# A third buffer for the weights, row adds moved to VectorE, and small products pinned late, in a hybrid attention and ConvFFN step

## The chip, the cores and the metric

The kernel runs on 1 core of one Trainium2 chip. The metric is the device time of one execution in microseconds, as the median of several runs. Its engines are TensorE (PE in the profile, its weight loads PEld), VectorE (DVE), ScalarE (ACT), GpSimd (POOL) and SyncE (SP), whose queue here issues the DMAs.

## The reference

One layer of a streaming encoder, all in float32, on 512 prompt tokens and 32 sample tokens with cached keys and values:

```
h = rmsnorm(x) * g1
qa, ka, va, qb, kb, vb, ga, gb = split(h @ w_in)        # 1024 -> 6656
oa = sliding window attention (16 heads, 4 kv heads, ALiBi, sink), q and k normed per head
ob = chunk band attention (16 heads, learned bias by distance), q and k normed per head
x = x + (sigmoid(ga) * oa + sigmoid(gb) * ob) @ w_out   # 1024 -> 1024
u = (rmsnorm(x) * g2) @ w_up                            # 1024 -> 2 * 2816
c = conv_b + conv_w0 * u[t-2] + conv_w1 * u[t-1] + conv_w2 * u[t]   # causal, per channel
x = x + (gelu(c[first half]) * c[second half]) @ w_down # 2816 -> 1024
```

For the sample tokens u[-2] and u[-1] come from a cached state (`cache_ffn_conv`). The new keys and values and the last rows of u are returned too.

## The kernel before

**Layout and arithmetic.** Activations lie transposed: 128 channels on the partitions, the T = 544 tokens along the row, in two halves of 272. To keep float32 precision each operand of a matmul is split into a rounded high part and the rest, a low part, and each product is made of three matmuls: high x high, high x low, low x high (`triple`, L220).

**Weights.** A weight tile is 128 x 1024 (8 blocks of 128 x 128, one output block of 128 channels for all of D = 1024). `prep` (L192) takes three tiles from the pool `wp`: `w_raw` (loaded by SyncE), `w_hi` (cast by GpSimd up to the end of w_out, by ScalarE from w_up on) and `w_lo` (a subtraction on VectorE). The pool has two buffers of each. `weights()` (L213) hands out the next tile and sees that the tiles up to two behind it are begun. What `prep_next` issues has a lower priority by 300 places than what stands around it. There are 50 tiles of w_in, 8 of w_out, 44 of w_up, 6 of w_down; `dense` (L232) uses one of them in 48 matmuls (2 halves, 8 blocks, 3 each). All loads that go through `load` (L166) with the same kind keep their written order in SyncE's queue.

**Order of the work.** Instructions are traced in an order that a small planner (`Stream`, L69) sets for TensorE: between dense products it steps through attention tasks when their estimated latencies are over. A scheduler then orders each engine's queue by readiness in a simulated time, and by priority; engines work their queues off in that order.

**Start.** x is loaded in 8 row blocks, interleaved with the first two weight tiles. Each row block k is split into xh and xl at once (`row_split`, ScalarE and VectorE), without its norm: the first FIRST = 3 tiles are multiplied by x times gain only (`dense_first`, L271), and their six halves stay in six PSUM banks until rstd is there. `RowNorm.row` (L337) squares each x block on ScalarE and adds it to a running sum on the engine given (L398: GpSimd for blocks up to 4, VectorE for the rest); `finish` splits the sum and multiplies it by a matrix of ones, and rstd is made on ScalarE and VectorE (L312, L360, L361). Up to the eighth tile VectorE multiplies each result by rstd as it leaves PSUM (L290); then x itself is rescaled (L254) and split again (L327).

**ConvFFN.** 44 tiles of w_up, each followed by the convolution on VectorE, ScalarE and a few GpSimd instructions on `carry`, six small products of the cached state with the convolution's weights (L925 to L929) that depend on inputs alone. Gate and value products are split and kept. Of the 22 products the first REST = 6 are used directly; 16 form 8 pairs, whose seven factors (`make_pair`, L960) serve a Strassen-like form of w_down. EARLY pairs are made as soon as their products are there, the others behind the last gate. A split half of a pair or product lives in a home: first the 19 slots of pool `gp`, then slots of `fp`, then the 16 tiles of xh and xl once w_up is through, then `fp` again. Pool `fp` has 50 slots of 128 x 544, in which x1 (8 slots) and working tiles lie as well.

**End.** First the 6 direct products (48 blocks of w_down), then the pairs: for each of four pairs of output rows (m), 4 units of 7 factors, each factor 6 matmuls. `sums` (L1007) loads a unit's weights, forms s13, s2 and s4 with three VectorE additions, and casts and subtracts each of the seven operands into a slot of `fp` (L1020, L1021), traced up to 10 operands ahead. Behind the last unit of each m the seven PSUM banks are combined into x1 and stored (`leave`, L1072).

Of the kernel before, what the change touches and what calls it, by code (L numbers as in the profile page):

```python
# [8 lines left out]
F32 = mybir.dt.float32  # L9
F32R = mybir.dt.float32r  # L10
AF = mybir.ActivationFunctionType
ALU = mybir.AluOpType
# [14 lines left out]
GT = FF // 128  # L27
PAIRS = 8
REST = GT - 2 * PAIRS
EARLY = 5  # L30
UNITS = PAIRS // 2
H = T // 2
EPS = 1e-6
# [110 lines left out]
def body(ctx, tc, a, o):  # L144
# [4 lines left out]
    V, G = nc.vector, nc.gpsimd  # L149
    rr = lambda t: t.bitcast(F32)  # L150

    const = ctx.enter_context(tc.tile_pool(name="const", bufs=1))
    wp = ctx.enter_context(tc.tile_pool(name="wp", bufs=2))
    xp = ctx.enter_context(tc.tile_pool(name="xp", bufs=1))
    psd = ctx.enter_context(tc.tile_pool(name="psd", bufs=3, space=PSUM))
    psa = ctx.enter_context(tc.tile_pool(name="psa", bufs=5, space=PSUM))
# [9 lines left out]
    def load(out, src, kind="x"):  # L166

        with tc.issue_after(loads[kind].ins) if kind in loads else nullcontext():
            loads[kind] = nc.sync.dma_start(out=out, in_=src)
# [13 lines left out]
    sources = [a["w_in"][m] for m in plan] + [a["w_out"][m] for m in range(8)]  # L183
# [6 lines left out]
    state = {"prepped": 0, "used": 0}  # L190

    def prep(n):  # L192
        raw = wp.tile([128, 1024], F32, name="w_raw", bufs=2)
        hi = wp.tile([128, 1024], F32R, name="w_hi")
        lo = wp.tile([128, 1024], F32R, name="w_lo")
        W[n] = (hi, lo)
        cuts = (0, 256, 1024) if n < 2 else (0, 1024)
        for c in map(slice, cuts, cuts[1:]):
            load(raw[:, c], sources[n][:, c])
            if n < ffn:  # L200
                G.tensor_scalar(hi[:, c], raw[:, c], 1.0, 1.0, ALU.mult, ALU.mult)  # L201
            else:
                nc.scalar.copy(hi[:, c], raw[:, c])  # L203
            V.tensor_tensor(lo[:, c], raw[:, c], rr(hi)[:, c], ALU.subtract)  # L204
            yield

    def prep_next():
        with tc.high_priority(LATER):
            for _ in prep(state["prepped"]):
                pass  # L210
        state["prepped"] += 1

    def weights():  # L213
        n = state["used"]
        state["used"] += 1
        while state["prepped"] < min(n + 3, len(sources)):
            prep_next()
        return W.pop(n)

# [12 lines left out]
    def dense(evac, pool=None):  # L232
        if not norm_done:
            return dense_first(evac)
        if early:
            pool = psa
            early.clear()
        w = weights()
        for s, (c0, cn) in enumerate(HALVES):
            ps = bank(pool or psd)  # L240
            for k in range(KC):
                triple(ps, w, k, c0, cn, k == 0, k == KC - 1)
                if k == KC - 1:
                    evac(s, c0, cn, ps[:, :cn])
                if xt:
                    rescale(state["used"], s, k)
                pe.step()
# [23 lines left out]
    def dense_first(evac):  # L271


        early.append((evac, weights()))
        if len(early) < (FIRST if xt else 2):
            return
        halves = [(bank(psd if i < 3 else psa), early[i // 2][1], i % 2) for i in range(2 * len(early))]
        interleaved(halves[:3], range(KC))
        for h in halves[3:]:
            interleaved([h], range(KC))  # L280
        while not norm_done:
            pe.idle()
        for i, (ps, _, s) in enumerate(halves):
            c0, cn = HALVES[s]
            early[i // 2][0](s, c0, cn, ps[:, :cn])
# [80 lines left out]
    att = ctx.enter_context(ExitStack())  # L366
# [9 lines left out]
    xt = [slot() for _ in range(KC)]  # L376
    load(n1, a["n1"])
    w = [prep(0), prep(1)]
    for step in START.split():
        n = int(step[1])  # L380
# [14 lines left out]
    norm = RowNorm(sp, ap)  # L395
    rstd = norm.r
    for k in range(KC):
        norm.row(xt[k], G if k <= 4 else V)  # L398


    def head_norm(gi, write):
# [468 lines left out]

    lag = 2
    w0, w1 = weights(), weights()
    halves = [(bank(psd), w0, 0), (bank(psd), w0, 1), (bank(psd), w1, 0), (bank(psa), w1, 1)]
    for k in range(KC):
# [8 lines left out]
    interleaved(halves[3:], range(KC))  # L883
    att.close()

    fp = att.enter_context(tc.tile_pool(name="fp", bufs=50, reuse_waits="tile"))
    ft = att.enter_context(tc.tile_pool(name="ft", bufs=1, reuse_waits="tile"))
    x1 = [fp.tile([128, T], F32, name="s") for _ in range(KC)]
    for m in range(KC):
# [1 line left out]
    norm = RowNorm(fp, ft)  # L891
# [29 lines left out]
    carry = ft.tile([128, UT, 2], F32, name="carry")  # L921
    per = lambda name: cols[:, slice(*COL[name])]
    state_c = per("cc").rearrange("p (m r) -> p m r", r=2)
    t = ft.tile([128, UT], F32, name="t_c")
    for r in range(2):  # L925
        G.tensor_tensor(carry[:, :, r], per("cw0"), state_c[:, :, r], ALU.mult)
        G.tensor_tensor(carry[:, :, r], carry[:, :, r], per("cb"), ALU.add)
    G.tensor_tensor(t, per("cw1"), state_c[:, :, 1], ALU.mult)
    G.tensor_tensor(carry[:, :, 0], carry[:, :, 0], t, ALU.add)  # L929

    def conv(m, n, done):
        u = us[n % 2]
# [20 lines left out]
    rest, pairs = [], []  # L953
    homes = [gp] * 19 + [fp] * (7 * EARLY + 2 * REST - 19) + [f"x{p}{k}" for k in range(KC) for p in "hl"]

# [4 lines left out]
    def make_pair(v1, v2):  # L960
        b11, b12, b21, b22 = (v[:, c:c + H] for v in (v1, v2) for c in (0, H))
        t13, t24 = (fp.tile([128, T], F32, name="s") for _ in range(2))
        first, *wide = home(), (home(), home()), (home(), home()), (home(), home())
        nc.scalar.copy(first[:, :H], b11)
        V.tensor_tensor(first[:, H:], b11, rr(first)[:, :H], ALU.subtract)
        split(*wide[0], v2)
        V.tensor_tensor(t13[:, :H], b11, b12, ALU.subtract)
        V.tensor_tensor(t13[:, H:], b12, b22, ALU.subtract)
        split(*wide[1], t13)
        V.tensor_tensor(t24[:, :H], b22, t13[:, :H], ALU.add)  # L970
        V.tensor_tensor(t24[:, H:], b21, t24[:, :H], ALU.subtract)
        split(*wide[2], t24)
        ops = {"b11": (first[:, :H], first[:, H:])}
        for names, hl in zip((("b21", "b22"), ("t1", "t3"), ("t2", "t4")), wide):
            for e, name in enumerate(names):
                ops[name] = tuple(x[:, e * H:e * H + H] for x in hl)
        pairs.append(ops)

    late = []
    for n, i in enumerate(gate_order):  # L980
# [6 lines left out]
        def gate(c, part=part, n=n):  # L987
# [7 lines left out]
            late.append(v)  # L995
            if n % 2 and len(pairs) < EARLY:
                make_pair(*late)
# [8 lines left out]

    def sums():  # L1007
        for n in range(KC // 2 * UNITS):
            raw = wp.tile([128, 1024], F32, name="w_raw", bufs=2)
            load(raw, a["w_pair"][n])  # L1010
            wc, wd, wa, wb = (raw[:, 256 * e:256 * e + 256] for e in range(4))
            s13, s24 = (fp.tile([128, 2, 256], F32, name="s") for _ in range(2))
            s1, s3, s2, s4 = s13[:, 0], s13[:, 1], s24[:, 0], s24[:, 1]
            V.tensor_tensor(s13, raw[:, 256:768].rearrange("p (e c) -> p e c", e=2),
                            wc.unsqueeze(1).to_broadcast([128, 2, 256]), ALU.add)
            V.tensor_tensor(s2, s1, wa, ALU.add)
            V.tensor_tensor(s4, s2, wb, ALU.add)
            for x in (wa, s2, s3, s1, wb, wd, s4):
                w = fp.tile([128, 2, 256], F32R, name="s")
                nc.scalar.copy(w[:, 0], x)  # L1020
                V.tensor_tensor(w[:, 1], x, rr(w)[:, 0], ALU.subtract)  # L1021
                ready.append(w)
                yield

    ready = []
    making = sums()

    def operand(n, ahead=10):
# [203 lines left out]
```

## Time and profile before

| | |
|---|---|
| median of 3 runs | 923.89 us (923.56 to 924.41) |
| profiled execution | 924.88 us, span 923.0 us |
| TensorE busy | 898.6 us (97%), 7085 matmuls |
| VectorE busy | 723.6 us (78%), 1471 instructions |
| ScalarE busy | 542.2 us (59%) |
| GpSimd busy | 379.1 us (41%), 578 instructions |
| chain that ended last, by engine | PE 76%, DVE 9%, ACT 4%, POOL 3%, issue 2% |

Times count from the start of the span. A busy share of TensorE counts overlapping matmuls, so it tells idle time and not speed. "Idle before" with an engine's name is the time that an engine stood still ahead of an instruction, and what released it.

### The profile page before, as it was taken

What the parts mean: (1) busy time and instruction counts of PE and PEld (TensorE: products, weight loads), DVE (VectorE), ACT (ScalarE), POOL (GpSimd) and SP (SyncE); (2) the same over time, 40 slices, a digit from 0 to 9 for tenths busy, and PEclk for the clock granted to TensorE, in tenths of its full rate; (3) what the DMA queues carried; (4) which work ended last, traced back from release to release, by engine and by line L of the source; (5) the groups of instructions that cost most, each with busy time, mean ns of one, the idle gap of its engine ahead of it and who ended that gap; (6) DMA issues with size and microseconds to landing.
All of it is one profiled execution on the core that took longest, in us unless ns stands there. A gap on an engine that the chain in (4) does not pass through costs nothing.

```text
span 923.0 us, 18908 instructions
## 1 busy us (share of the span) xinstructions
PE 898.6 (97%) x7085; PEld 884.4 (96%) x7085; DVE 723.6 (78%) x1471; ACT 542.2 (59%) x1285; POOL 379.1 (41%) x578
## 2 busy tenths in 40 slices
PE   8879999999999999999999999999999999999998
PEld 7879899989989999999999999999999999999998
DVE  7799876868888888998866558768777776886996
ACT  5568777778878777777764244344444443534542
POOL 6534457465876777766541103221222221100100
PEclk9999999999999999999999999999999999999999
DMA  6222222322334443434415222222222222332342
GB/s 216 83 82 88 71 90 85 101 81 75 109 118 122 135 124 109 129 110 136 133 59 168 89 92 92 92 77 85 92 93 92 84 87 83 96 101 81 119 145 67
DMA packets 40012, 94.38 MB, mean 102 GB/s; under 512 B 4944, under 2 KB 16240, under 8 KB 39920
## 3 DMA queue, kind: packets, MB, share of 16 engines
q1 hardware_dynamic: 39920, 93.17, 31.8%
q8 instruction: 56, 0.92, 0.4%
q14 instruction: 36, 0.29, 0.1%
HBM read 80.48 MB, written 7.10 MB: 95 GB/s over the span
## 4 chain that ended last, share of the span: by engine, by line
PE 76%; DVE 9%; ACT 4%; POOL 3%; issue 2%; DMA 0%; DVEq 0%; POOLq 0%
PE ps L85 73%; PE ps L89 3%; ACT p L485 2%; DVE q L446 1%; DVE zn L422 1%; DVE p L501 1%; DVE w_lo L204 1%; POOL p L493 1%; DVE s L254 1%; DVE t_b L319 1%; DVE k L431 1%; POOL t_sql L414 1%; POOL z L421 1%; DVE pt_l L512 0%; DMA k<-k 0%
## 5 line engine op out<-in xcount | busy, mean ns | idle before, releaser
L85 PE MATMUL ps<-xh,w_lo 128*128 128x272 f32 x1536 | 446.3, 292 | 5.1 <-DVE w_lo L204 5.1
L85 PE MATMUL ps<-xh,w_hi 128*128 128x272 f32 x1536 | 446.0, 292 | 2.7 <-ACT z L412 1.7
L85 PE MATMUL ps<-xl,w_hi 128*128 128x272 f32 x1536 | 446.3, 291 | 0.8 <-DVE xl L327 0.8
L85 PEld LDWEIGHTS ps<-xh,w_lo 128*128 128x128 f32 x1536 | 291.6, 190 | 6.5 <-DVE w_lo L204 6.0
L85 PEld LDWEIGHTS ps<-xh,w_hi 128*128 128x128 f32 x1536 | 291.5, 190 | 4.8 <-ACT z L412 1.9
L85 PEld LDWEIGHTS ps<-xl,w_hi 128*128 128x128 f32 x1536 | 292.0, 190 | 2.1 <-DVE xl L327 1.7
L204 DVE TENSOR_TENSOR w_lo<-w_raw,w_hi 128x1024 fp32r<-128x1024 f32 (+2 forms) x112 | 143.2, 1279 | 30.8 <-ACT w_hi L203 18.3
L201 POOL TENSOR_SCALAR w_hi<-w_raw 128x1024 fp32r<-128x1024 f32 (+2 forms) x62 | 66.6, 1075 | 90.2 <-PE ps L85 70.3
L493 POOL TENSOR_SCALAR p<-p,rc 128x256 f32<-128x256 f32 (+3 forms) x128 | 74.2, 596 | 41.4 <-DVE rc L491 38.0
L203 ACT CAST w_hi<-w_raw 128x1024 fp32r<-128x1024 f32 x50 | 52.6, 1051 | 64.9 <-issue 36.1
L85 PE MATMUL ps<-s,w_hi 128*128 128x272 f32 x448 | 84.0, 288 | 0.0
L485 ACT ACTIVATE p<-p,nm 128x256 f32<-128x256 f32 (+3 forms) x128 | 65.4, 514 | 27.8 <-DVE nm L482 27.7
L938 POOL TENSOR_SCALAR state_u<-u 128x2 f32<-128x2 f32 x44 | 17.1, 388 | 148.7 <-DVE u L935 148.7
L85 PE MATMUL ps<-s 128*128 128x272 f32 (+1 forms) x483 | 71.3, 293 | 1.7 <-DVE s L372 1.7
L85 PEld LDWEIGHTS ps<-s,w_hi 128*128 128x128 f32 x448 | 70.1, 188 | 0.0
L935 DVE TENSOR_TENSOR u<-ps,rstd 128x272 f32<-128x272 f32 x88 | 38.5, 441 | 39.6 <-PE ps L85 37.0
L85 PEld LDWEIGHTS ps<-s 128*128 128x128 f32 x483 | 65.1, 190 | 2.2 <-DVE s L372 1.7
L85 PE MATMUL ps<-s,w_lo 128*128 128x272 f32 x224 | 63.8, 288 | 0.0
L85 PE MATMUL ps<-k,q 128*128 128x256 f32 (+2 forms) x256 | 52.1, 308 | 3.5 <-DMA k<-k 1.8
L414 POOL TENSOR_TENSOR t_sql<-t_sq,t_sqh 128x272 fp32r<-128x272 f32 x52 | 52.7, 1014 | 3.7
L421 POOL TENSOR_TENSOR z<-z,t_y 128x272 f32<-128x272 f32 x52 | 42.7, 822 | 23.9 <-ACT t_y L316 21.7
L512 DVE TENSOR_TENSOR pt_l<-ps,pt_h 128x512 fp32r<-128x512 f32 (+1 forms) x80 | 45.6, 602 | 5.5 <-ACT pt_h L511 4.4
(166 smaller groups left out, 1635.1 us busy)
## 6 DMA issues: line engine op xcount, KB each, us to landing
w_raw<-in_w_in SPq DMA_DIRECT2D x50, 512.0 KB, 3.4
w_raw<-in_w_up SPq DMA_DIRECT2D x44, 512.0 KB, 3.3
w_raw<-in_w_pair SPq DMA_DIRECT2D x16, 512.0 KB, 3.4
k<-k SPq DMA_DIRECT2D x40, 128.0 KB, 2.3
bias<-in_rel SPq DMA_DIRECT2D x16, 256.0 KB, 2.7
w_raw<-in_w_out SPq DMA_DIRECT2D x8, 512.0 KB, 3.5
s<-in_x SPq DMA_DIRECT2D x15, 272.0 KB, 5.7
w_raw<-in_w_down SPq DMA_DIRECT2D x6, 512.0 KB, 3.3
```

Of the source, the lines that this page charges most:

```text
L85: return self.nc.tensor.matmul(out, lhsT=lhsT, rhs=rhs, **kw)
L89: return self.nc.tensor.transpose(out, src, ident)
L201: G.tensor_scalar(hi[:, c], raw[:, c], 1.0, 1.0, ALU.mult, ALU.mult)
L203: nc.scalar.copy(hi[:, c], raw[:, c])
L204: V.tensor_tensor(lo[:, c], raw[:, c], rr(hi)[:, c], ALU.subtract)
L414: G.tensor_tensor(sql, sq, rr(sqh), ALU.subtract)
L421: G.tensor_tensor(z, z, y, ALU.mult)
L485: act(p[:, sl], p[:, sl], AF.Exp, bias=nm[:, t:t + 1], accum_out=sm[:, t:t + 1])
L493: G.tensor_scalar(p[:, sl], p[:, sl], rc[:, t:t + 1], 1.0, ALU.mult, ALU.mult)
L512: V.tensor_tensor(l[:, :n], ps[:, :n], rr(h)[:, :n], ALU.subtract)
L935: V.tensor_tensor(u[:, 2 + c0:2 + c0 + cn], ps, rstd2[:, c0:c0 + cn], ALU.mult)
L938: G.tensor_scalar(state_u[:, m, 0:2], u[:, NP:NP + 2], 1.0, 1.0, ALU.mult, ALU.mult)
```

## The change

Three buffers instead of two for w_raw, w_hi and w_lo (12 KB more of each SBUF partition); each `weights()` begins tiles up to three behind the one handed out. The `fp` pool shrinks from 50 to 44 slots, EARLY from 5 to 4, and the sums of the pair weights move from two `fp` slots into a buffer of `w_lo`. All seven adds of the squares of x run on VectorE. The six small products on GpSimd are each pinned behind what was traced before on that engine.

```diff
-EARLY = 5
+EARLY = 4
...
-    wp = ctx.enter_context(tc.tile_pool(name="wp", bufs=2))
+    wp = ctx.enter_context(tc.tile_pool(name="wp", bufs=3))
...
-        raw = wp.tile([128, 1024], F32, name="w_raw", bufs=2)
+        raw = wp.tile([128, 1024], F32, name="w_raw")
...
-        while state["prepped"] < min(n + 3, len(sources)):
+        while state["prepped"] < min(n + 4, len(sources)):
...
-        norm.row(xt[k], G if k <= 4 else V)
+        norm.row(xt[k], V)
...
-    fp = att.enter_context(tc.tile_pool(name="fp", bufs=50, reuse_waits="tile"))
+    fp = att.enter_context(tc.tile_pool(name="fp", bufs=44, reuse_waits="tile"))
...
+    late_g = lambda *x: tc.keep_in_program_order(G.tensor_tensor(*x))
     for r in range(2):
-        G.tensor_tensor(carry[:, :, r], per("cw0"), state_c[:, :, r], ALU.mult)
-        G.tensor_tensor(carry[:, :, r], carry[:, :, r], per("cb"), ALU.add)
-    G.tensor_tensor(t, per("cw1"), state_c[:, :, 1], ALU.mult)
-    G.tensor_tensor(carry[:, :, 0], carry[:, :, 0], t, ALU.add)
+        late_g(carry[:, :, r], per("cw0"), state_c[:, :, r], ALU.mult)
+        late_g(carry[:, :, r], carry[:, :, r], per("cb"), ALU.add)
+    late_g(t, per("cw1"), state_c[:, :, 1], ALU.mult)
+    late_g(carry[:, :, 0], carry[:, :, 0], t, ALU.add)
...
-            raw = wp.tile([128, 1024], F32, name="w_raw", bufs=2)
+            raw = wp.tile([128, 1024], F32, name="w_raw")
...
-            s13, s24 = (fp.tile([128, 2, 256], F32, name="s") for _ in range(2))
+            both = wp.tile([128, 4, 256], F32, name="w_lo")
+            s13, s24 = both[:, 0:2], both[:, 2:4]
```

## Rows read from the trace of the kernel before

**Rows 1.** The page's first part: busy us, share, instructions.

```profile
PE 898.6 (97%) x7085; PEld 884.4 (96%) x7085; DVE 723.6 (78%) x1471; ACT 542.2 (59%) x1285; POOL 379.1 (41%) x578
```

**Rows 2.** Stretches: length, busy PE, PEld, DVE, ACT, POOL, granted clock, DMA, GB/s.

```profile
12.00:24.00 12.00, 10.18 (x71) 8.85 (x69) 11.43 (x12) 5.71 (x11) 11.69 (x12) 1.00 0.52 172
24.00:36.00 12.00, 9.85 (x61) 9.39 (x62) 8.82 (x15) 5.06 (x13) 5.19 (x7) 0.86 0.35 106
...
60.00:72.00 12.00, 9.07 (x63) 8.85 (x62) 11.73 (x30) 9.92 (x23) 1.04 (x1) 0.89 0.18 55
...
480.00:560.00 80.00, 80.00 (x638) 79.92 (x637) 49.97 (x77) 32.92 (x49) 12.79 (x19) 1.00 0.34 114
```

**Rows 3.** TensorE's timeline: start, us, instruction, idle before it and its releaser.

```profile
24.26 0.52 PE L85 MATMUL ps<-s,ones 128*128 128x272 f32 x2 [0.51 <-ACT s L351]
25.21 0.40 PE L85 MATMUL ps<-xh,w_hi 128*128 128x272 f32 x1 [0.43 <-POOL w_hi L201]
27.76 0.40 PE L85 MATMUL ps<-xh,w_lo 128*128 128x272 f32 x1 [1.46 <-DVE w_lo L204]
...
51.07 0.37 PE L85 MATMUL ps<-t_sqh,bdiag 128*128 128x272 f32 x1 [1.42 <-POOL w_hi L201]
...
69.08 0.44 PE L85 MATMUL ps<-xh,w_lo 128*128 128x272 f32 x1 [2.93 <-DVE w_lo L204]
```

**Rows 4.** Stretches of 2 us, columns as in rows 2.

```profile
28.00:30.00 2.00, 2.00 (x12) 2.00 (x12) 2.00 (x5) 0.35 (x2) 0.00 (x0) 0.58 0.58 182
...
32.00:34.00 2.00, 2.00 (x18) 2.00 (x17) 0.62 (x2) 1.91 (x5) 1.25 (x3) 1.00 0.35 131
...
70.00:72.00 2.00, 2.00 (x10) 2.00 (x10) 2.00 (x7) 1.83 (x5) 0.00 (x0) 0.50 0.85 264
```

**Rows 5.** GpSimd's timeline at the start, columns as in rows 3.

```profile
13.20 5.64 POOL L342 TENSOR_TENSOR s<-s 128x544 f32<-128x544 f32 x3
18.81 1.48 POOL L926 TENSOR_TENSOR carry<-cols 128x44 f32<-128x44 f32 x2
...
24.11 2.52 POOL L201 TENSOR_SCALAR w_hi<-w_raw 128x1024 fp32r<-128x1024 f32 x2
...
35.01 1.05 POOL L201 TENSOR_SCALAR w_hi<-w_raw 128x1024 fp32r<-128x1024 f32 x1 [1.68 <-PE ps L85]
```

**Rows 6.** Instructions on tile s, 0 to 40 us: duration ns min/median/max, starts, forms.

```profile
L327 DVE SCALAR_TENSOR_TENSOR xl<-s,n,xh x9: 501/795/1880, 4.3 to 20.1; 128x544 fp32r<-128x544 f32 x7, 128x272 fp32r<-128x272 f32 x2
...
L342 POOL TENSOR_TENSOR s<-s x4: 1356/1764/1960, 10.4 to 17.1; 128x544 f32<-128x544 f32 x4
...
L342 DVE TENSOR_TENSOR s<-s x3: 712/800/976, 20.8 to 22.7; 128x544 f32<-128x544 f32 x3
```

**Rows 7.** VectorE's timeline at the start, columns as in rows 3.

```profile
15.76 5.11 DVE L327 SCALAR_TENSOR_TENSOR xl<-s,n,xh 128x544 fp32r<-128x544 f32 x4
...
21.92 1.62 DVE L342 TENSOR_TENSOR s<-s 128x544 f32<-128x544 f32 x2
...
30.28 0.50 DVE L361 TENSOR_SCALAR rstd<-rstd 128x272 f32<-128x272 f32 x2
```

**Rows 8.** Timelines of TensorE, ScalarE and VectorE in the pair products.

```profile
835.40 11.06 PE L85 MATMUL ps<-s 128*128 128x272 f32 x87
...
836.36 0.41 ACT L1020 CAST s<-w_raw 128x256 fp32r<-128x256 f32 x1 [9.69 <-PE ps L85]
...
843.56 0.42 DVE L1021 TENSOR_TENSOR s<-s 128x256 fp32r<-128x256 f32 x1 [0.32 <-ACT s L1020]
...
846.16 0.68 DVE L1014 TENSOR_TENSOR s<-w_raw 128x512 f32<-128x512 f32 x1
```

**Rows 9.** VectorE's groups, 800 to 835 us: busy us, mean ns, idle before.

```profile
L204 DVE TENSOR_TENSOR w_lo<-w_raw,w_hi 128x1024 fp32r<-128x1024 f32 x5 | 6.1, 1223 | 1.1 <-ACT w_hi L203 1.1
...
L431 DVE TENSOR_TENSOR xl<-s,xh 128x544 fp32r<-128x544 f32 x3 | 2.2, 719 | 0.0
```

**Rows 10.** GpSimd's timeline as the convolutions begin.

```profile
551.03 0.19 POOL L938 TENSOR_SCALAR state_u<-u 128x2 f32<-128x2 f32 x1 [27.74 <-DVE u L935]
```

## The prediction

> **What bounds the kernel now.** I read the page's busy shares first, then the stretches, then TensorE's waits, then the queues of the engines it waits for. TensorE is busy 898.6 of 923.0 us, so the idle time there, 24.4 us, is nearly all that can be won [rows 1]. The stretches show where it lies: from 480 us on TensorE is never idle (80.00 of 80.00 us in the row shown), so nothing that the change does there can save time, it can only cost. In 12 to 24, 24 to 36 and 60 to 72 us it is idle for 1.82, 2.15 and 2.93 us [rows 2]. In the timeline each long gap of the first 84 us names a weight tile or the row sum: 0.51 us for the sum (L351), 0.43 and 1.46 us for the high and low part of the third tile, 1.42 us for a high part at 51 us, 2.93 us for a low part at 69 us [rows 3]. Two of these gaps cost more than themselves: behind them the granted clock falls to 0.58 and 0.50, which is about its lower level of 1.2 GHz, and TensorE starts 12 and 10 matmuls in 2 us where it starts 18 at 1.00 [rows 4].
>
> Why are the weights late? Two buffers: the third tile's high part goes where the first tile's was, so GpSimd can't cast it before TensorE has left the first tile. And GpSimd is then still behind: three of its row adds fill 13.20 to 18.84, the small products for the cached state follow at 18.81, and the cast starts at 24.11 [rows 5]. VectorE is slowed at the same time.
>
> **Part 1: the start, 8 to 36 us.** Third buffer: the third tile needs no release, so its load, cast and subtraction run while TensorE works on the first two. Removed on GpSimd in this stretch: 4 row adds (median 1.764 us each, [rows 6]) and six small products. Added on VectorE: 4 adds at 0.800 us (median, [rows 6]), 3.2 us. But a VectorE instruction with two operands in SBUF is slow while GpSimd adds: four xl back to back take 5.11 us, 1.28 us each [rows 7], against a median of 0.795 [rows 6]. So VectorE gets back some 0.48 us in each of five xl, 2.4 us, and more in two low parts: its load hardly rises. The Trainium skill (SBUF — State Buffer, "Who interferes with whom") says of this that such an instruction and a GpSimd instruction that reads SBUF exclude each other, the later one waiting for the whole of the other. By that rule each moved add gives VectorE 1.76 us and costs it 0.80, and the sum below would be 0.9 us larger (all of 1.82 us instead of half); the rows lie between.
>
> From rows: VectorE from 10.4 us on has two low parts of 768 columns (estimate 0.92 each, three quarters of the 1.22 us that 1024 take later, [rows 9]), five xl (4.0), seven adds (5.6) and the third tile's low part (1.2): 12.6 us, to about 23 us; with the ends of successive instructions overlapping, 22. The sum ends now at 21.92 + 1.62 = 23.54 and rstd at 30.28 + 0.50 = 30.78 [rows 7]. After: rstd at about 28.5 to 30. Its first readers hold six of the eight PSUM banks, so TensorE can't go far past the third tile without it. TensorE leaves that tile now at about 34.9 (the cast at 35.01 waits for it, [rows 5]).
>
> What TensorE wins: the gaps of 0.51 + 0.43 + 1.46 = 2.40 us [rows 3]; the low clock behind them, two slices of 2 us (the second, with 11 starts, is like the first) with 6 + 7 = 13 starts fewer than 18 each, at 0.125 us (80 us / 638, [rows 2]) 1.6 us; and of the 1.82 us idle in 12 to 24, which xl and low parts cause, half: 0.9. Sum 4.9 us; the third tile would then end at 30.0, just behind rstd. Bounds: 5.8 if all of it goes; at the other end the adds stand before an xl and the sum is no earlier, see the first rival.
>
> **Part 2: 48 to 84 us, the tiles begun one earlier.** The gaps of 1.42 and 2.93 us [rows 3] and the low clock behind the second, 8 starts fewer in 70 to 72 and an estimated 2 more beside it, 10 × 0.125 = 1.2 us [rows 4], are 5.6 us. The wait there was in fact VectorE's backlog: it is busy 11.73 of 12 us [rows 2]. A buffer moves its 1.2 us for a low part ahead, it doesn't remove it; what stands behind then comes later, and attention matmuls will wait for q, p or zn. I take half: 2.8 us. Bounds 5.6 and -1 (a low part put before a q that TensorE needs sooner costs up to its 1.2 us). From 84 to 480 us no gap that the waits name is a weight's; the order of the queues will shift a little with the new tiles, for which I take 0, bounds -2 and +2.
>
> SyncE: loads stay in their written order. A fourth tile's load waits for the first tile's raw buffer, the one that a third tile's load waited for: the same low part releases it, one tile sooner. The loads of x behind it move no later.
>
> **Part 3: small products late.** Pinned behind the last traced GpSimd cast, the one of the last w_out tile, all six come at some time past 500 us. GpSimd is idle there for 27.74 us before its first use of u at 551.03 [rows 10], and the carry is read behind that. Cost 0; if that cover were gone, a few tenths.
>
> **Part 4: the end, where SBUF is paid for.** The third buffers take 12 KB of each partition; fp gives up 6 slots of 2176 B. EARLY = 4 leaves four pairs, not three, to make after the last gate: one more pair is 4 subtractions and 3 splits on VectorE, 0.43 × 5 + 0.72 × 3 = 4.3 us (0.72 from [rows 9], 0.43 estimated as the same rate with half the columns and a fixed part), in 800 to 835 us, where VectorE has idle time and TensorE works on the rest blocks. Cost 0; without the cover at most 4.3.
>
> The products are another thing. Count fp there, before: x1 8, homes 28 + 5 = 33, so 50 - 41 = 9 slots, 2 for the sums and 7 for ready operands; the trace agrees, seven are cast and then ScalarE waits 9.69 us, until TensorE leaves the first operand at 836.36 [rows 8]. After: homes 21 + 12 = 33 as well, so 44 - 41 = 3, all for operands since the sums now live in w_lo. An operand's slot is held: first matmul 835.40 to release 836.36, 0.96; cast 0.41; subtraction 0.42; with an estimated 0.1 for handing on 1.9 us in all [rows 8]. Three slots give one operand each 0.63 us, TensorE takes 6 × 0.125 = 0.75. It holds, with 0.37 us to spare per operand (0.62 as the low part comes two matmuls in). A sum instruction of 0.68 us [rows 8] before it on VectorE uses that up, and so do the nine evacuations at the end of the first pair of rows. Later it eases: each stored pair of rows frees 2 slots. So 28 operands are at stake. None late: 0. Each behind a 0.68: (1.9 + 0.68)/3 - 0.75 = 0.11, 3.1 us. With only two slots, because the last pair still holds one for its temporaries: 1.9/2 - 0.75 = 0.20, 5.6 us. I take 1.3, nearer to none since most operands meet no sum.
>
> **Sum.** 4.9 + 2.8 + 0 - 1.3 = 6.4 us. The profiled execution took 924.88 us, its span 923.0 and 1.88 around it; after, 918.5. It lies 0.99 above the median of the runs, 923.89, so I forecast 917.5 for the median.
>
> **Rivals.**
> First: VectorE becomes the bound of the start. For: it is busy 11.43 of 12 us in 12 to 24 [rows 2]. Against: the slowed xl. If the xl stay slow, the adds come on top, the sum ends 3.2 us later, rstd at 34.0, and TensorE waits from 30.0 to then: the 4.9 shrink to 0.9. Time 923.89 - 0.9 - 2.8 + 1.3 = 921.5. The Trainium skill (Perfetto Trace Analysis, "Optimizing Scalar/DVE Operations") advises moving work off a saturated VectorE, which this change reverses; it warns in the same place that GpSimd shares a port with it. Chance 0.12.
> Second, slower: three operand slots are too few. Decides from the point where an operand is held up on VectorE by more than 0.37 us; two slots and a 0.68 in front of each give (1.9 + 0.68)/2 - 0.75 = 0.54 us per operand, 15 us over 28 operands: 923.89 - 7.7 + 15 = 931.2. For: the slots can be counted. Against: sums can run ahead, they have three buffers. Chance 0.10.
> Third: the buffers change nothing, since VectorE's backlog is the cause everywhere and the queues' order shifts gaps to other matmuls. Gains of 2 to 3 against the 1.3 to 3.1 of the products: 923.5. Chance 0.11.
> Fourth: all of both stretches: 5.8 + 5.6 and nothing lost at the end: 912.5. Chance 0.10.
> The forecast, 914 to 920.5, has the other 0.57.
>
> **Numbers.** The range 912.5 to 924.0 leaves out the second rival and the edges of the third and fourth, about 2 in 10; the likeliest case's own is 914 to 920.5. Within 0.2% (1.85 us), about what a measurement of this kernel can tell from no change, lies the third rival; slower is the second and a little of the third.
>
> **What would show it.** Right: no row add and no small product on GpSimd before 30 us, the third tile's low part done before 24 us, no wait for w_lo or w_hi behind 20 us, a granted clock of 1.00 through 28 to 32 and 70 to 72, TensorE idle 18 to 21 us instead of 24.4, and ScalarE's operand casts waiting for TensorE one by one. Wrong: new TensorE gaps from 835 us on of more than 3 us in sum, rstd later than 31 us, or gaps of the same size in 48 to 120 us under other names.

## The result

The changed kernel takes 939.46 us (median of 4 runs, 939.04 to 940.49) against 923.72 us for the kernel before (four runs, with one more than above): ratio 1.0174, interval 1.0156 to 1.0191. It is slower by 16 us; I had forecast 917.5, and my range ended at 924.0. The profiled execution has a span of 937.3 us. The page's first part, in the form of [rows 1]:

```profile
PE 902.9 (96%) x7085; PEld 883.0 (94%) x7085; DVE 725.8 (77%) x1475; ACT 543.0 (58%) x1285; POOL 371.6 (40%) x574
```

TensorE's idle time rose from 24.4 to 34.4 us. The stretches of [rows 2], and the one behind 72 us:

```profile
12.00:24.00 12.00, 9.08 (x68) 8.40 (x66) 11.82 (x15) 5.12 (x10) 6.08 (x6) 1.00 0.70 234
24.00:36.00 12.00, 9.87 (x66) 9.88 (x67) 6.95 (x10) 2.79 (x7) 1.94 (x2) 0.86 0.37 123
...
60.00:72.00 12.00, 11.27 (x85) 10.39 (x84) 11.84 (x27) 9.51 (x17) 2.31 (x2) 1.00 0.18 55
72.00:84.00 12.00, 9.56 (x49) 8.70 (x50) 11.84 (x31) 9.51 (x26) 2.29 (x3) 0.72 0.19 63
480.00:560.00 80.00, 79.17 (x642) 78.14 (x641) 48.09 (x73) 35.78 (x67) 19.45 (x23) 1.00 0.32 107
```

The stretch of 72 to 84 us in the kernel before:

```profile
72.00:84.00 12.00, 11.93 (x90) 11.24 (x89) 12.00 (x27) 10.61 (x27) 5.96 (x7) 0.97 0.25 70
```

60 to 72 us starts 85 matmuls where it started 63, and 72 to 84 us then 49 where the kernel before starts 90. VectorE is full in both stretches, before (11.73 and 12.00 of 12 us) and after (11.84 in both): its backlog stayed, and TensorE's wait for it moved by one stretch.

To place the loss I sum, over each stretch, by how much the distance from one matmul's start to the next exceeds what the first one's columns take at full clock (0.125 us for 272, and no less than 0.11 for a small one; excesses below some 0.04 us are left out). This **gap sum** holds idle time and the cost of the lower clock together:

| us | 0-48 | 48-84 | 84-120 | 120-480 | 480-830 | from 830 | all |
|---|---|---|---|---|---|---|---|
| before | 13.1 | 8.6 | 4.5 | 23.7 | 0.1 | 0.0 | 50.0 |
| after | 12.3 | 9.6 | 4.2 | 31.5 | 2.3 | 3.9 | 63.8 |

The 13.8 us more are 7.8 in the attention stage, 2.2 in its last tasks, behind 480 us, 3.9 in the pair products and 1.0 in 48 to 84 us; the start gives back 0.8. Those last two are too small to be told from nothing: e_slots6 below has the kernel's old order on all four compute engines up to 480 us, and its gap sums of the first four stretches are 13.2, 7.9, 2.9 and 24.7, up to 1.6 us away from those before. The waits of TensorE from 48 to 480 us say what it waits for there (total, times, longest). Before:

```profile
PE ps L85 <- DVE w_lo L204: 2.9, 1, 2.9
PE ps L89 <- DVE t_b L319: 1.9, 1, 1.9
...
PE ps L85 <- POOL w_hi L201: 1.4, 1, 1.4
...
PE ps L85 <- DVE s L520: 0.8, 1, 0.8
...
PE ps L85 <- DVE pt_l L512: 0.6, 2, 0.3
PE ps L85 <- DVE q L446: 0.5, 1, 0.5
```

After:

```profile
PE ps L89 <- DVE t_b L319: 3.2, 3, 1.6
PE ps L85 <- DVE s L520: 2.8, 3, 1.1
PE ps L85 <- DVE q L446: 2.5, 2, 1.3
PE ps L85 <- DVE pt_l L512: 2.3, 4, 1.0
PE ps L89 <- DVE pt_l L512: 2.2, 4, 0.8
PE ps L85 <- DVE xl L327: 2.1, 1, 2.1
```

The two weights are gone from the list, as the buffers promised. In their place stand operands of attention (q, pt_l, s, t_b), more and longer.

The start, VectorE's timeline (start, us, instruction), to hold against [rows 7]:

```profile
21.23 1.22 DVE L204 TENSOR_TENSOR w_lo<-w_raw,w_hi 128x1024 fp32r<-128x1024 f32 x1
22.36 3.03 DVE L342 TENSOR_TENSOR s<-s 128x544 f32<-128x544 f32 x2
25.32 1.21 DVE L204 TENSOR_TENSOR w_lo<-w_raw,w_hi 128x1024 fp32r<-128x1024 f32 x1
26.45 0.71 DVE L352 TENSOR_TENSOR s<-s 128x544 fp32r<-128x544 f32 x1
...
35.70 0.50 DVE L361 TENSOR_SCALAR rstd<-rstd 128x272 f32<-128x272 f32 x2
```

The third tile's low part is done at 22.45, as forecast, but it stands ahead of the last two row adds. Those take 1.5 us each beside GpSimd's casts of two more tiles (21.93, first view below), and the row sum ends at 25.39 (23.54 before). TensorE waits 3.72 us for its high half (second view). The low half is multiplied by the ones only 25 dense matmuls later, at 31.14 (in the kernel before at 25.82), and rstd comes at 36.2 (30.78 before).

```profile
21.93 2.89 POOL L201 TENSOR_SCALAR w_hi<-w_raw 128x1024 fp32r<-128x1024 f32 x2 [1.35 <-DVE gains L394]
```
```profile
26.13 0.53 PE L85 MATMUL ps<-s,ones 128*128 128x272 f32 x2 [3.72 <-ACT s L351]
...
31.14 0.41 PE L85 MATMUL ps<-s,ones 128*128 128x272 f32 x2
...
74.65 0.59 PE L85 MATMUL ps<-xl,w_hi 128*128 128x272 f32 x1 [2.12 <-DVE xl L327]
...
845.85 10.64 PE L85 MATMUL ps<-s 128*128 128x272 f32 x84
...
865.72 1.02 PE L85 MATMUL ps<-s 128*128 128x272 f32 x6 [0.80 <-DVE s L1023]
```

At the end ScalarE casts three operands and then waits 9.82 us for TensorE (seven and 9.69 in [rows 8]); from there on a few products wait for theirs, the longest 0.80 us at 865.72.

```profile
836.56 0.41 ACT L1022 CAST s<-w_lo 128x256 fp32r<-128x256 f32 x1 [0.18 <-DVE s L431]
846.79 0.41 ACT L1022 CAST s<-w_lo 128x256 fp32r<-128x256 f32 x1 [9.82 <-PE ps L85]
```

### The profile page after: what moved, and what is told of

It reads as the page before. It is cut to its first block, busy times and chain, and to the rows that moved or that the text cites. A ratio compares the mean times of both kernels' runs of the same rounds, so it can differ in the third digit from the quotient of the medians.

```text
span 937.3 us, 18983 instructions
## 1 busy us (share of the span) xinstructions
PE 902.9 (96%) x7085; PEld 883.0 (94%) x7085; DVE 725.8 (77%) x1475; ACT 543.0 (58%) x1285; POOL 371.6 (40%) x574
## 3 DMA queue, kind: packets, MB, share of 16 engines
q1 hardware_dynamic: 39920, 93.17, 31.2%
## 5 line engine op out<-in xcount | busy, mean ns | idle before, releaser
L204 DVE TENSOR_TENSOR w_lo<-w_raw,w_hi 128x1024 fp32r<-128x1024 f32 (+2 forms) x112 | 140.7, 1256 | 37.7 <-ACT w_hi L203 19.5
L201 POOL TENSOR_SCALAR w_hi<-w_raw 128x1024 fp32r<-128x1024 f32 (+2 forms) x62 | 70.3, 1135 | 93.2 <-PE ps L85 63.9
L485 ACT ACTIVATE p<-p,nm 128x256 f32<-128x256 f32 (+3 forms) x128 | 65.4, 514 | 24.9 <-DVE nm L482 24.7
L85 PE MATMUL ps<-s 128*128 128x272 f32 (+1 forms) x483 | 68.1, 295 | 2.8 <-DVE s L372 1.7
L85 PE MATMUL ps<-k,q 128*128 128x256 f32 (+2 forms) x256 | 55.5, 311 | 5.8 <-DVE q L446 2.5
L421 POOL TENSOR_TENSOR z<-z,t_y 128x272 f32<-128x272 f32 x52 | 46.8, 903 | 19.6 <-ACT t_y L316 17.2
L89 PE MATMUL ps<-ident,p 128*128 128x128 f32 x272 | 46.3, 276 | 5.8 <-DVE t_b L319 3.2
L430 ACT CAST s<-s 128x544 fp32r<-128x544 f32 x31 | 20.0, 645 | 51.1 <-DVE s L990 26.8
```

The costliest lines, as they stand in the source:

```text
L85: return self.nc.tensor.matmul(out, lhsT=lhsT, rhs=rhs, **kw)
L89: return self.nc.tensor.transpose(out, src, ident)
L421: G.tensor_tensor(z, z, y, ALU.mult)
L430: nc.scalar.copy(dst_hi, src)
L485: act(p[:, sl], p[:, sl], AF.Exp, bias=nm[:, t:t + 1], accum_out=sm[:, t:t + 1])
```

## The experiments

"Gap" is the gap sum of 120 to 480 us and that from 830 us on. Ratios are to runs of the kernel before on the same chip. Its medians there are 922.8 to 924.9 us, so times of runs that stand in different groups below can differ by up to 2 us for the chip alone; the ratios allow for that.

| run | what it is | us | ratio (interval) | gap |
|---|---|---|---|---|
| e_late | before + late small products | 921.86 | 0.9976 (0.9961 to 0.999) | 23.9, 0 |
| e_adds | before + adds on VectorE | 923.07 | 0.9986 (0.9971 to 1.0) | 23.9, 0 |
| e_both | both of these | 923.81 | 0.9989 (0.9975 to 1.0003) | 24.1, 0 |
| e_mem | before + the end: fp 44, EARLY 4, sums in w_lo | 926.56 | 1.002 (1.0004 to 1.0035) | 23.8, 3.5 |
| e_slots6 | the same with fp 47 | 924.0 | 1.0 (0.9982 to 1.0018) | 24.8, 0 |
| e_fp3 | e_mem + third buffers, begun as before | 939.15 | 1.0148 (1.0127 to 1.0168) | 28.7, 3.8 |
| e_buf | e_fp3 + begun one earlier | 938.82 | 1.0149 (1.0128 to 1.017) | 28.8, 3.3 |
| e_n3 | after, begun as before | 940.04 | 1.0161 (1.0142 to 1.018) | 31.2, 3.7 |
| o_all | e_fp3, all queues in e_mem's order | 926.15 | 1.0037 (1.0022 to 1.0052) | 24.1, 1.9 |
| o_fp3 | e_fp3, TensorE in e_mem's order | 928.47 | 1.0063 (1.0047 to 1.0079) | 23.6, 3.6 |
| o_after | after, TensorE in e_mem's order | 929.54 | 1.0068 (1.0045 to 1.009) | 23.6, 3.6 |
| o_rev | e_mem, TensorE in e_fp3's order | 942.88 | 1.0218 (1.0199 to 1.0237) | 29.2, 4.1 |
| p_mem | e_mem, TensorE in written order | 1014.05 | 1.0964 (1.0932 to 1.0995) | 70.7, 4.3 |
| p_fp3 | e_fp3, the same | 1017.42 | 1.1008 (1.0981 to 1.1034) | 70.7, 4.4 |
| p_after | after, the same | 1017.58 | 1.1003 (1.0968 to 1.1037) | 69.8, 4.0 |
| a_start | after, the start's order mended | 937.94 | 1.0157 (1.0137 to 1.0178) | 32.6, 4.1 |
| t1 | e_late, 16 waits filled | 922.3 | 0.9989 (0.9975 to 1.0003) | 22.7, 0 |
| t2 | e_late, 6 of them filled | 922.25 | 0.998 (0.9964 to 0.9995) | 22.9, 0 |

**One part at a time: e_late, e_adds, e_mem, e_buf.** Each is the kernel before with those lines of the change alone.

> The kernel before, with the six small products alone pinned late. If the loss lies in the buffers or in the adds, this is within 2 us of before (922 to 926), and the cast of the third weight tile starts earlier than 24.11 us. If the pinned products were the cause, it is above 930.

> The kernel before, with all adds of squares on VectorE alone. If the adds are the cause (a later row sum, a later rstd, everything behind it late), some 930 or more and the row sum is cast later than 23.57 us. If GpSimd's adds slowed VectorE as the prediction said, 919 to 923 and the cast at 22 to 23 us.

> The kernel before with fp at 44 slots, EARLY = 4 and the sums in w_lo, but two buffers as before. If three operand slots cost what the pair products lost in the changed kernel, 927 to 928 (4 us more), with nothing changed before 480 us. If the end costs only what I predicted, 925.

> All of the buffers: third buffers, begun four ahead, fp 44, EARLY 4, sums in w_lo; adds and small products as before. If the buffers and what they do to the order of the queues in the attention part are the cause, 936 to 941, with 8 to 12 us lost between 120 and 480 us. If the adds are, 920 to 927.

The loss is in e_buf, and not at its end: e_mem, the same end with two buffers, is 12 us faster. e_mem does more than its lines say: without any pin its small products move as well, from 18.81 to 483.9 us, so it has the gain of e_late too, and against that run its end costs 4.7 us. The same move is in e_buf, e_fp3 and the other kernels made from these. e_adds shows what the adds alone do, on VectorE:

```profile
20.18 1.61 DVE L342 TENSOR_TENSOR s<-s 128x544 f32<-128x544 f32 x2
...
28.80 0.50 DVE L361 TENSOR_SCALAR rstd<-rstd 128x272 f32<-128x272 f32 x2
```

The row sum ends at 21.79 (forecast 22) and rstd is there at 29.3 (forecast 28.5 to 30). Its six xl from 8 to 24 us average 0.79 us where the seven of the kernel before average 1.18: VectorE did get back what GpSimd's adds had cost it. In the time little of it is left: the interval of the ratio ends at 1.0.

**Which line of the buffers: e_fp3, e_n3; and the end: e_slots6, e_both.**

```diff
-wp = tc.tile_pool(name="wp", bufs=2)     # e_fp3 on e_mem; raw likewise
+wp = tc.tile_pool(name="wp", bufs=3)
-while prepped < min(n + 4, ...)          # e_n3 on after
+while prepped < min(n + 3, ...)
```

> As the run with all of the buffers (938.8), but tiles begun three ahead as before: three buffers, so a cast in GpSimd's queue finds its buffer free and needs no wait for TensorE. Theory: the loss comes from casts that stand at the head of GpSimd's queue and wait for TensorE to leave a tile, with the attention part's work behind them; then this is 925 to 929, near the run with fp 44 alone (926.6), and GpSimd's wait for TensorE before casts between 120 and 480 us is below 10 us. Rival: any third buffer lets the weights be made too early and crowd out the attention part's work on VectorE and GpSimd; then 935 to 940.

> The changed kernel (adds on VectorE and small products late as well), but tiles begun three ahead. By the first theory 922 to 927, as its small parts each gained 1 to 2 us; by the rival 935 to 940.

> The kernel before with EARLY = 4 and the sums in w_lo, two buffers, and fp at 47 slots: six operand slots at the end instead of three. If the slots are what costs 4 us at the end, 921 to 923; if the fourth late pair or the sums in w_lo is, 926 to 927 as with three slots.

> The kernel before with the adds on VectorE and the small products late, buffers as before. If the two gains (2.2 and 1.3 us) are of different stretches, 920 to 921; if both come from the same free place on GpSimd in the first 30 us, 921.5 to 923.

Beginning tiles earlier is not it: e_fp3 is as slow as e_buf. My theory of that time, casts that wait at the head of GpSimd's queue because they are begun four ahead, fell with it. A third buffer alone costs 12.6 us (939.15 against 926.56). e_n3 does gain at the start (gap sum to 48 us 9.8, against 13.1 before) and is no faster than the other two. At the end six operand slots have no gap sum, three have 3.5 us: the slots are that cost, though the time of e_slots6, 924.0, lies above the 921 to 923 expected; its small products stay at the start, at 19.0 us. e_late and e_adds don't add up: e_both is above either of its forecasts.

**The order of the queues.** Nothing in e_fp3 is more work. But the scheduler sees weights ready sooner in its simulated time and orders every queue anew: against e_mem 2494 of TensorE's 7021 instructions stand elsewhere, by up to 61 places. In the kernel before 267 dense matmuls stand ahead of the first of k and q, in the changed kernel 295; the first transpose of p, the probabilities of attention, starts at 80.2 us before, 88.7 after, 94.3 in e_fp3. First I held TensorE to the order in which the code writes it:

```diff
+pe.pin = tc.keep_in_program_order      # around each matmul and transpose
```

> The kernel of e_mem (two weight buffers, fp of 44, EARLY of 4, sums in w_lo) with every TensorE instruction kept in the order in which the code writes it; in e_mem the scheduler orders TensorE's queue by when it reckons operands ready. It is the base for the next two runs. All theories: same computation, another order of TensorE's queue, between 915 and 960 us; no theory says more of it, the differences to it count.

> p_mem with third buffers for the weights, begun three ahead as before; TensorE's queue is the same instruction by instruction in both. Between e_fp3 and e_mem, where the order was free, the third buffers cost 12.6 us. Theory A (the buffers let the scheduler place dense matmuls ahead of attention's in TensorE's queue, and that order costs the time): within 3 us of p_mem, or faster. Rival B (weight preparation stands earlier in VectorE's and GpSimd's queues and delays attention's operands there, whatever TensorE's order): 8 to 14 us above p_mem. Rival C (the bytes themselves: other addresses, more traffic at a time): 8 to 14 us above p_mem as well.

> The changed kernel (third buffers, four ahead, adds on VectorE, late small products) with TensorE's queue in written order, the same as in p_mem. Theory A: 0 to 6 us below p_mem, since the weights' waits go and nothing is paid for them in the order; rstd at or before 33 us, where the changed kernel has 36.2. Rivals B and C: 8 to 15 us above p_mem, rstd at about 36.

The difference shrinks from 12.6 to 3.4 us, about as theory A has it, though p_after, expected 0 to 6 us below p_mem, is 3.5 us above. But the written order itself costs 88 us, and with a gap sum of 70 us in the attention stage its waits may cover anything. So I gave kernels the order of another kernel's queues, instruction by instruction:

```diff
+for p, n in zip(order, order[1:]):    # order: e_mem's queue, by number
+    tc.add_manual_dep(traced[n], p, NoSync)
```

> e_fp3 (third weight buffers, begun three ahead), with the queues of TensorE, VectorE, ScalarE, GpSimd and SyncE all in exactly the order that they have in e_mem, its two-buffer counterpart at 926.56 us; only the buffers and the waits for them differ. Theory A (the order that the scheduler gives TensorE costs the 12.6 us) and rival B (its order of VectorE and GpSimd costs them): 923 to 928 us, no slower than e_mem, and the waits for weights between 48 and 84 us shorter. Rival C (the buffers themselves, their addresses or traffic): 935 to 941.

> e_fp3 with TensorE's queue alone in e_mem's order; VectorE, ScalarE and GpSimd are ordered afresh by the scheduler, with weight casts and subtractions earlier. Theory A: 924 to 930 us. Rival B: 934 to 940 us, as e_fp3. If both orders carry a part, in between.

> The reverse: e_mem, two buffers, with TensorE's queue in e_fp3's order (2494 of 7021 TensorE instructions stand elsewhere, by up to 61 places). Theory A: 934 to 944 us, slow without any third buffer. Rival B: 924 to 930 us.

> The whole change with TensorE's queue in e_mem's order instead of its own. Theory A: 921 to 929 us, of which 3 to 4 are the three operand slots of the last stage, and rstd before 33 us where the changed kernel has 36.2. Rivals B and C: 934 to 941 us.

This settles that the order is the cause. Three buffers with every queue in the old order cost nothing that is clear of the intervals (o_all 926.15 and 1.0037, e_mem 926.56 and 1.002). With TensorE alone in the old order 10.7 of the 12.6 us are back by the medians, and by the ratios two thirds of the loss (1.0063, between 1.0148 and 1.002). Two buffers in the new order are slow (o_rev 942.88); that run alone would not show it, since in 48 to 120 us it waits 7.2 us for low parts of weights, in an order made for three buffers. Under the whole change the old order of TensorE's queue takes back 9.9 of its 15.7 us (o_after, just above the 921 to 929 expected). Rival C is out within the intervals, and B as the main cause: o_fp3 is 2.3 us above o_all on the same chip, which the other queues' order can account for. The gap sum of 120 to 480 us follows TensorE's order in every run that has one of the two: 23.6 to 24.8 with the old, 28.7 to 32.6 with the new. In the changed kernel that stretch and the tasks behind it hold the loss; in e_fp3, against e_mem, they hold only some 5.5 of 13.6 us, and 7.8 lie ahead of 120 us.

o_all also shows that the buffers win nothing even so. Its TensorE waits, 48 to 480 us (the order list shifts its line numbers; these are w_lo and w_hi of `prep`):

```profile
PE ps L358 <- DVE w_lo L477: 2.9, 1, 2.9
...
PE ps L358 <- POOL w_hi L474: 1.4, 1, 1.4
```

The same 2.9 and 1.4 us as before, with a buffer more and the old order, where I had expected shorter ones: what was late there was the work on VectorE and GpSimd.

**Are the waits themselves the price, and the start: t1, a_start, t2.**

> e_late (two buffers, late small products, 921.86 us) with all queues in its own order, except that 16 times between 50 and 410 us, where its trace shows TensorE waiting 0.2 to 1.9 us for an operand of attention, the dense matmuls that follow within 70 places in an already begun sum are put ahead of the waiting one: 102 of them are pulled forward, as many as the wait is long. The waits concerned add up to 9.6 us of cover. Theory A (the order of TensorE's queue sets what its stalls cost): 912 to 918 us. Rival (attention's chain on VectorE and ScalarE is itself late, and a stall filled here comes back at a later place): 919 to 923 us.

> The changed kernel with all queues in its own order, except at the start: on VectorE the last two row adds stand ahead of the low part of the third tile (the changed kernel has them behind it), and the low half of the row sum ahead of the fourth tile's low part; on TensorE the second pair of matmuls with the ones stands 6 dense matmuls behind the first pair, not 25. If the order on VectorE made the row sum late: the row sum ends at 24.0 to 24.5 us (25.39 in the changed kernel), rstd is there at 30.5 to 32.5 (36.2). Time, if a gain at the start reaches the end: 934 to 937.5 us. Rival, VectorE's backlog in 60 to 84 us takes it back: 938 to 941.

> e_late in its own order on all queues, with only the six waits of attention at 181, 191, 195, 206, 374 and 403 us filled, by 29 dense matmuls that follow them. In t1 the excess of those two stretches fell by 2.2 us and that of others rose by as much. If filling helps where the chain has slack: 919 to 921 us, 1 to 3 us under e_late's 921.86. If a filled stall always returns later: 921.5 to 923 us.

a_start, VectorE and then TensorE:

```profile
20.95 2.30 DVE L615 TENSOR_TENSOR s<-s 128x544 f32<-128x544 f32 x2
23.17 2.05 DVE L477 TENSOR_TENSOR w_lo<-w_raw,w_hi 128x1024 fp32r<-128x1024 f32 x1
```
```profile
23.98 0.52 PE L358 MATMUL ps<-s,ones 128*128 128x272 f32 x2 [1.88 <-ACT s L624]
```

The row sum ends at 23.25, 2.1 us earlier than in the changed kernel, rstd at 30.7: the places of those few instructions were that delay. The time falls by 1.5 us (937.94), which the intervals do not tell from nothing. At 48 us it is 8 dense matmuls ahead of the changed kernel (254 against 246, 1 us), at 480 us 3: nearly all is taken back.

t1 fell on its rival. It filled waits that add up to 9.6 us and gained nothing; the gap sum of 120 to 480 us is 22.7 instead of 23.9, that of 48 to 120 us 13.0 instead of 9.9. t2, with the six best places, is no faster either. Moving dense work in front of a waiting attention matmul did not pay here.

What the traces do show is when attention begins and ends. The transposes of p (tile p: duration ns min/median/max, first and last start, forms), before, after, e_mem and e_fp3:

```profile
L89 PE MATMUL ps<-ident,p x272: 270/272/329, 80.2 to 479.1; 128*128 128x128 f32 x136
L89 PE MATMUL ps<-ident,p x272: 270/272/332, 88.7 to 491.6; 128*128 128x128 f32 x136
...
L89 PE MATMUL ps<-ident,p x272: 270/272/332, 78.5 to 475.8; 128*128 128x128 f32 x136
L89 PE MATMUL ps<-ident,p x272: 270/272/329, 94.3 to 489.2; 128*128 128x128 f32 x136
```

e_fp3 starts 472 dense matmuls ahead of the first of them, e_mem 413. Those 59 take 7.4 us at full clock, and as many fewer are left to stand between attention's matmuls; yet the stretch is hardly shorter (394.9 us against 397.3). Attention's last matmul comes 13.6 us later (495.8 against 482.2), and from there to the end both take 441 us. In the changed kernel it comes 12.2 us later than before (497.6 against 485.4). This fits a late beginning of attention that nothing behind it makes up. It is argued from the traces and not shown: no run moves that beginning alone, and p_mem, which begins at 69.1 us, takes 489 us for the stretch. Which of the 2494 places carry the 12 us is open.

The fastest version that the runs show is e_late, 0.9976 of the kernel before, with t2 (0.998) inside its interval: two buffers, and of the change the late small products alone.

## Why the prediction was wrong

- **84 to 480 us, the step that failed.** I wrote: "the order of the queues will shift a little with the new tiles, for which I take 0, bounds -2 and +2". It cost 7.5 us there (4.5 + 23.7 to 4.2 + 31.5) and 2.2 behind 480 us. o_fp3 and o_after show that the order of TensorE's queue is the cause of most of it. I had looked at the edits' own instructions for costs; this one issues none.
- **Part 2, +2.8.** Measured -1.0 (gap sum 8.6 to 9.6), which is not told from 0. I had seen that VectorE is full there [rows 2] and halved the gain for it; o_all shows that in the old order none was due, as both waits stay with a buffer more. In the changed kernel the two waits do go, and the wait for xl at 74.65 is one of those that I had coming later in their place.
- **Part 1, +4.9.** Measured +0.8, no more than two executions of one order differ by. The adds were right: e_adds has the row sum and rstd where I put them. That a third buffer also puts the third tile's low part ahead of the last adds, and two casts beside them, I had as the far end of a bound ("the adds stand before an xl and the sum is no earlier"), for another reason. That the low half of the sum would wait behind 25 dense matmuls I had nowhere. rstd at 36.2 is what I had named as wrong, "later than 31 us". Even where the start went well, in e_n3 with 3.3 us, none of it reached the end. Of the Trainium skill's rule (SBUF — State Buffer, "Who interferes with whom"), that a VectorE instruction with two inputs in SBUF and a GpSimd instruction that reads SBUF exclude each other, the runs agree on the direction: without GpSimd's adds an xl takes 0.39 us less, and two row adds beside GpSimd's casts took 3.03 instead of 1.61 us. One pair comes near it in size: a low part of 768 columns that began just behind a GpSimd add of 1.36 us took 2.10 us in the kernel before, and 0.96 in e_adds without the add.
- **Part 3, 0.** They cost nothing, as I had it, and gained what I had not put in the sum: e_late is 2 us faster than the kernel before, clear of its interval; GpSimd begins its next cast at 23.60 us there instead of 24.11 [rows 5].
- **Part 4, -1.3.** Measured -3.9, inside its bounds of 0 and 5.6: the three slots were counted rightly and the mechanism is shown by e_slots6; I took too small a share of operands that wait. The second rival's 15 us did not come.
- **Rivals.** The third came nearest, with "the queues' order shifts gaps to other matmuls", but priced the shift at nothing. No case of mine let it cost 10 us.

## What to carry to other kernels

Where a scheduler orders the queues by simulated readiness, a buffer more is an edit of every queue: compare the order of the kernels' queues before crediting it, and impose the old order on the new kernel to tell the resource from the order. A wait for a tile need not be a lack of buffers: here the engine that makes the tile was busy 11.7 of 12 us. A gain at the start need not reach the end: here a_start's, small as it is, was nearly gone by 480 us, behind stretches where VectorE is full.

## What was not expected of the hardware

VectorE became less loaded by taking over adds from GpSimd: its xl, row adds and low parts from 8 to 24 us take 15.1 us before (13 of them) and 12.5 us in e_adds (15 of them), and the row sum ends 1.75 us earlier. Of the rest the surprise is the size of what order alone does at equal work: 926 us, 943 us and 1014 us for the same instructions (e_mem, o_rev and p_mem).
